# One diffusion trunk layer: the prologue's hand order becomes a table of works

## The chip, the cores and the metric

The kernel runs on one core of a Trainium2 chip. The metric is the device time of one execution in microseconds; lower is better. Engines are named TensorE (PE; PEld is its weight load), VectorE (DVE), ScalarE (ACT), GpSimd (POOL) and SyncE (SP, which issues nearly all DMAs here).

## The reference

One layer for 128 context tokens and 512 latent tokens, 640 rows of 1024 channels. Cut to what the change touches:

```python
ada = silu(c) @ w_ada + b_ada              # c for latent tokens, c_ctx for context tokens
sh1, sc1, g1, sh2, sc2, g2 = split(ada, 6)
u = rms_norm(h, g_pre1) * (1 + sc1) + sh1
z = u @ w_in                               # q 1024, k 256, v 256, then five parts of 1024
k = rms_norm(k, k_norm); keys = concat(cache_k, rope(k)); vals = concat(cache_v, v)
att = softmax(q keys^T / 8) vals           # context reads only context
```

Behind it come a gated convolution, an output projection and a convolutional feed-forward layer, all unchanged. Arithmetic is in float32: a float32 product is made of three products of rounded parts, high x high, high x low and low x high.

## The kernel before

**What the prologue has to make.** Tokens are five tiles t = 0 to 4 of 128 rows (tile 0 is the context), channels eight blocks f = 0 to 7 of 128. The prologue runs from the start to about 57 us and ends with k and v of all tiles, in five PSUM banks, one per tile, each summed over the eight channel blocks. The steps:

- x: load the tile (`XT`), square and sum (ScalarE, L434), factor (`rstd_of`, POOL, L281 and L282), normalise (VectorE, L439, `xn`), turn it by eight TensorE transposes (L446), copy it to `xT` (L452 on ScalarE, L454 on VectorE; two halves of four blocks each).
- small rows: c, c_ctx, b_ada and g_pre1 arrive as rows, are turned (L417), give the silu columns in `s32` (L418, L419) and the feature columns `feat` (L423, L425).
- modulation: for a group of one or two channel blocks the scale and shift columns of `w_ada` are loaded (two loads of 512 KB for a single block, four for a pair), multiplied (L477, 32 narrow matmul instructions for a single block, 64 for a pair), copied (L485), folded by another small product (L490, L493, L497) and put into `scsh` (L502, L504). `modulate` then writes for a block the high part `UH` (ScalarE, L519), the whole `u` (VectorE, L520) and the low part `UL` (VectorE, L523).
- k and v weights: unit u = 0 to 7 is channel block u of 512 columns of `w_in` (256 KB); `cut_upto` makes its high part (ScalarE, L200 or L591) and its low part (VectorE, L201 or L593). Units 8 and 9 are the first two of the q weights (512 KB). There are three slots for raw weights, two of the small units to a slot, and three slots for cut ones.
- product: `kv_mm(f, ts)` adds block f to tiles ts, three matmuls of 128x512 per tile (L235, L236, L237); `kv_first` does block 0 of tiles 0 to 2 (L530).
- rest: cached keys and values, rotary tables times the gains (L666 to L673), the cached keys turned (L546, L552, L553), the rows for the second norm (L681 to L684).

**What sets the order.** The order is written by hand: calls follow one another, and TensorE, ScalarE, VectorE and SP execute in exactly that order (`tc.manual_schedule`). Semaphores between engines come from the tiles' uses. A 32-transposition warm-up (L378) stands first on TensorE. Modulation groups are `((0,), (1,), (2, 3), (4, 5), (6,), (7,))`; those in `JOINT = (0, 3, 4, 5)` are multiplied at once when both parts have landed, groups 1 and 2 in two halves, scale and shift apart.

**What follows.** The attention stage is a list of works with needs (`work`, `Room`) whose order on all engines is the string `PLAN`, played by `follow`. A work names its engine, what it needs, and the rooms (banks, slots) that it uses; a figure behind a number picks the room, a letter picks the engine where there is a choice. PLAN begins with q products on TensorE, squares of k4, k2 and k3 on ScalarE (L871), the rotation of k1 on VectorE (L848, L849) and the addition belonging to it on POOL (L869). Then come projections and the feed-forward layer, which are nearly all matmuls (L1273).

Of the kernel before, what the change touches and what calls it, by code (L numbers as in the profile page):

```python
# [21 lines left out]
D = 1024  # L22
# [69 lines left out]
POOL_WAY = "11111111111111111111111101111100"  # L92

# [19 lines left out]
def trunk_layer(ctx, tc, x_prompt, x_sample, cache_k, cache_v, c, c_ctx, w_ada, b_ada, g_pre1, g_post1, g_pre2,  # L113
# [259 lines left out]
    with tc.tile_pool(name="pro", bufs=2) as pro, tc.manual_schedule(engines={mybir.EngineType.SP}):  # L373
        warm = pro.tile([128, 1], F32, name="warm", bufs=1)
        S.activation(warm, mhalf[:, 0:1], AF.Silu)
        wps = ps1()
        for _ in range(WARM):
            PE.transpose(wps[:, 0:128], ident, ident)  # L378

        def load_rows(srcs, eng):  # L380
            rows = pro.tile([72, 128], F32, tag="rows", name=nm("rows"), bufs=2)
            n = 0
            for src in srcs:
                m = src.shape[0] * src.shape[1] // 128
                eng.dma_start(rows[n:n + m, :], src.rearrange("o (k p) -> (o k) p", p=128))
                n += m
            return rows[0:n, :]

        rows1 = load_rows((c[0:1, :], c_ctx.unsqueeze(0), b_ada.unsqueeze(0), g_pre1), nc.scalar)


        GROUPS = ((0,), (1,), (2, 3), (4, 5), (6,), (7,))
        JOINT = (0, 3, 4, 5)
        araws = {}

        def araw_tile():
            return pro.tile([128, 1024], F32, tag="araw", name=nm("araw"), bufs=4)

        def ada_loads(g, rooms):
            n, c = len(GROUPS[g]), GROUPS[g][0] * 128  # L400
            araws[g] = rooms
            for i, raw in enumerate(rooms):
                o, k = (D, 0)[i // n], i % n * (KT // n)
                nc.sync.dma_start(raw.rearrange("p (k c) -> p k c", c=128 * n),
                                  w_ada[k * 128:(k + KT // n) * 128, o + c:o + c + 128 * n].rearrange("(k p) c -> p k c", p=128))

        XT = region(ra, "r3", [NT, D], F32, "XT")
        for t in range(NT):
            nc.sync.dma_start(XT[:, t, :], xrows(t))
        ada_loads(0, [araw_tile() for _ in range(2)])  # L410
        fetch(1)
        ada_loads(1, [araw_tile() for _ in range(2)])
        fetch(2)

        def features():
            ptr = ps1()
            PE.transpose(ptr[:, 0:72], rows1, ident[0:72, 0:72])  # L417
            S.activation(svec[:, :, 30], ptr[:, 0:8], AF.Silu)  # L418
            S.activation(svec[:, :, 31], ptr[:, 8:16], AF.Silu)  # L419
            return ptr  # L420

        def feature_columns():
            V.tensor_copy(feat[:, 0:72], ptr1[:, 0:72])  # L423
            for o in (8, 32):
                V.tensor_scalar(out=feat[:, F_B + o:F_B + o + 8], in0=feat[:, F_B + o:F_B + o + 8], scalar1=1.0, scalar2=None,  # L425
                                op0=ALU.add)

        xT = Halves(NTOK, F32, "xT")
        xns, rs, xps, pas, es = {}, {}, {}, {}, {}

        def square(t):
            junk = pro.tile([128, D], F32, tag="junk", name=nm("junk"), bufs=1)
            ssq = pro.tile([128, 1], F32, tag="ssq", name=nm("ssq"), bufs=NT)
            S.activation(junk, XT[:, t, :], AF.Square, accum_out=ssq)  # L434
            rs[t] = rstd_of(ssq, 1, 1.0 / D, pro)

        def normal(t):
            xns[t] = pro.tile([128, D], F32, tag="xn", name=nm("xn"), bufs=XB)
            V.tensor_scalar(out=xns[t], in0=XT[:, t, :], scalar1=rs[t], scalar2=None, op0=ALU.mult)  # L439

        def x_turn(t, ks=range(KT)):
            if ks[0] == 0:
                xps[t] = ps2()
            p = xps[t]
            for k in ks:
                PE.transpose(p[:, k * 128:(k + 1) * 128], xns[t][:, k * 128:(k + 1) * 128], ident)  # L446

        def x_copy(t, hf):
            src = xps[t].rearrange("p (k c) -> p k c", c=128)[:, 4 * hf:4 * hf + 4]
            dst = xT.half(hf)[:, :, t * 128:(t + 1) * 128]  # L450
            if t > 0 and hf == 0:
                S.activation(dst, src, AF.Copy)  # L452
            else:
                V.tensor_copy(dst, src)  # L454

        def ada1_mm(g, i):

            n = len(GROUPS[g])
            if i == 0:
                pas[g] = ps1()  # L460
            if g in JOINT and i == 0:
                return
            todo = []
            for kind in (0, 1) if g in JOINT else (i,):
                for f in range(n):
                    for k in range(KT):
                        if g not in JOINT:
                            j, k2 = (2 * f + k // 4, k % 4) if n == 2 else (k % 4, k // 4)
                            last = 3 if n == 2 else 1
                        else:  # L470
                            j, k2 = (2 * kind + f, k) if n == 2 else (2 * kind + k // 4, k % 4)
                            last = 7 if n == 2 else 3
                        raw, m = araws[g][kind * n + k * n // KT], (k % (KT // n) * n + f) * 128
                        todo.append((k2, j, k, raw[:, m:m + 128], last))
            c = 0 if g in JOINT else 128 * i
            for k2, j, k, x, last in sorted(todo, key=lambda z: z[:2]):
                PE.matmul(pas[g][32 * j:32 * j + 32, c:c + 128], s32[:, 32 * k + 30:32 * k + 62], x, start=k2 == 0, stop=k2 == last,  # L477
                          tile_position=(0, 32 * j))

        def ada1_copy(g, a=0, b=2):  # L480
            if a == 0:
                es[g] = pro.tile([128, 256], F32, tag="e", name=nm("e"))
            if g in JOINT:
                a, b = 0, 1
            S.activation(es[g][:, a * 128:b * 128], pas[g][:, a * 128:b * 128], AF.Copy)  # L485

        def ada1_fold(g):
            n, pa, e = len(GROUPS[g]), pas[g], es[g]
            if g in JOINT and n == 2:
                PE.transpose(pa[:, 256:384], e[:, 0:128], ident)  # L490
                at = lambda kind, f: 256 + 32 * (2 * kind + f)
            elif g in JOINT:
                PE.matmul(pa[:, 256:260], e[:, 0:128], sel2, start=True, stop=True)  # L493
                at = lambda kind, f: 256 + 2 * kind
            else:
                for kind in range(2):
                    PE.matmul(pa[:, 256 + 4 * kind:256 + 4 * kind + 2 * n], e[:, kind * 128:kind * 128 + 128], sel2 if n == 2 else sel[:, 0:2],  # L497
                              start=True, stop=True)
                at = lambda kind, f: 256 + 4 * kind + 2 * f
            for i, f in enumerate(GROUPS[g]):  # L500
                c0, c1 = at(0, i), at(1, i)
                V.tensor_scalar(out=scsh[:, f, 0:2], in0=pa[:, c0:c0 + 2], scalar1=feat[:, F_B + 8 + f:F_B + 9 + f],  # L502
                                scalar2=feat[:, F_PRE1 + f:F_PRE1 + 1 + f], op0=ALU.add, op1=ALU.mult)
                V.tensor_scalar(out=scsh[:, f, 2:4], in0=pa[:, c1:c1 + 2], scalar1=feat[:, F_B + f:F_B + 1 + f],  # L504
                                scalar2=None, op0=ALU.add)

        us = {}

        def modulate(f, a=0, b=NTOK, between=()):

            if a == 0:
                us[f] = pro.tile([128, NTOK], F32, tag="u", name=nm("u"))
            u = us[f]
            for i, (s0, s1) in ((1, SEGS[0]), (0, SEGS[1])):
                c, d = max(a, s0), min(b, s1)
                if c < d:

                    x, sc, sh = xT.at(f)[:, c:d], scsh[:, f, i:i + 1], scsh[:, f, 2 + i:3 + i]
                    S.activation(UH[:, f, c:d], x, AF.Identity, scale=sc, bias=sh)  # L519
                    V.tensor_scalar(out=u[:, c:d], in0=x, scalar1=sc, scalar2=sh, op0=ALU.mult, op1=ALU.add)  # L520
            for x in between:
                x()
            V.tensor_tensor(out=UL[:, f, a:b], in0=u[:, a:b], in1=UH[:, f, a:b].bitcast(F32), op=ALU.subtract)  # L523

        def kv_first(ts):

            wh, wl = state["cut"][0].at(0)
# [28 lines left out]
        for t in range(2):  # L556
            square(t)
# [1830 lines left out]
```

## Time and profile before

| | |
|---|---|
| median of 3 runs | 1079.62 us (1079.02 to 1079.99) |
| profiled execution: time / span | 1079.34 us / 1077.5 us |
| mean granted TensorE clock | 0.999 |
| busy over the span: PE, PEld, DVE, ACT, POOL | 99%, 92%, 81%, 54%, 12% |
| HBM read / written | 117.39 MB / 11.44 MB |
| first 40 us: DMA engines' busy share by 4 us | 0.55, 0.91, then 1.08 to 1.18 |
| attention, 57 to 235 us: PE / DVE / ACT busy | 22.5 to 25 of each 25 us at its densest (135 to 160 us) |

How to read it: times are microseconds from the span's start. A line of the timeline gives start, duration, engine, source line, operation, result <- operands, shapes, and in brackets how long the engine had been idle and what ended that. Starts of weight loads (PEld) follow one another more exactly than the matmuls, whose ends are modelled, so TensorE's list is measured by them. A line by stretches (from:to) gives for each engine the busy time and the instructions, then granted clock, DMA share and GB/s.

### The profile page before, as it was taken

What the parts mean: (1) busy time and instruction counts of PE and PEld (TensorE: products, weight loads), DVE (VectorE), ACT (ScalarE), POOL (GpSimd) and SP (SyncE); (2) the same over time, 40 slices, a digit from 0 to 9 for tenths busy, and PEclk for the clock granted to TensorE, in tenths of its full rate; (3) what the DMA queues carried; (4) which work ended last, traced back from release to release, by engine and by line L of the source; (5) the groups of instructions that cost most, each with busy time, mean ns of one, the idle gap of its engine ahead of it and who ended that gap; (6) DMA issues with size and microseconds to landing.
All of it is one profiled execution on the core that took longest, in us unless ns stands there. A gap on an engine that the chain in (4) does not pass through costs nothing.

```text
span 1077.5 us, 20246 instructions
## 1 busy us (share of the span) xinstructions
PE 1062.8 (99%) x8066; PEld 992.2 (92%) x8066; DVE 870.3 (81%) x1328; ACT 583.1 (54%) x1050; POOL 130.8 (12%) x162
## 2 busy tenths in 40 slices
PE   8999999999999999999999999999999999999997
PEld 6788898899999999999998789999999999998886
DVE  5699899855498999896599678889998998989544
ACT  5478999942344554445322466655555654555432
POOL 1087676500000000000000020000000000000001
PEclk9999999999999999999999999999999999999999
DMA  9829999962244333233667634333443443326722
GB/s 316 260 80 175 190 172 180 194 144 60 78 123 124 98 94 94 79 89 100 184 191 257 196 122 137 111 103 104 130 134 112 130 127 106 116 91 210 266 77 98
DMA packets 238444, 152.17 MB, mean 141 GB/s; under 512 B 94602, under 2 KB 215942, under 8 KB 238350
## 3 DMA queue, kind: packets, MB, share of 16 engines
q1 hardware_dynamic: 238238, 150.84, 51.6%
q8 instruction: 63, 1.03, 0.4%
q14 instruction: 31, 0.25, 0.1%
q10 hardware_dynamic: 112, 0.04, 0.0%
HBM read 117.39 MB, written 11.44 MB: 120 GB/s over the span
## 4 chain that ended last, share of the span: by engine, by line
PE 89%; DVE 3%; DMA 3%; ACT 2%; POOL 1%; issue 1%; SPq 0%; DVEq 0%; ACTq 0%; POOLq 0%
PE b L1273 47%; PE b L235 10%; PE b L237 10%; PE b L236 10%; PE s L708 3%; PE s L1072 2%; PE s L1169 2%; DMA araw<-in_w_ada_dram 1%; DMA PT<-P 1%; PE s L235 1%; PE s L237 1%; PE s L477 1%; DMA XT<-in_w_ada_dram 1%; DVE marks L1119 1%; ACT P L1133 1%
## 5 line engine op out<-in xcount | busy, mean ns | idle before, releaser
L1273 PE MATMUL b<-ZBr,whi 128*128 128x320 f32 x688 | 152.2, 309 | 0.0
L1273 PE MATMUL b<-MT,whi 128*128 128x320 f32 x608 | 134.3, 308 | 0.0
L1273 PEld LDWEIGHTS b<-ZBr,whi 128*128 128x128 f32 x688 | 115.0, 188 | 0.1
L1273 PE MATMUL b<-ZBr,wlo 128*128 128x320 f32 x344 | 106.2, 309 | 0.0
L1273 PEld LDWEIGHTS b<-MT,whi 128*128 128x128 f32 x608 | 101.6, 187 | 0.0
L1273 PE MATMUL b<-MT,wlo 128*128 128x320 f32 x304 | 93.6, 308 | 0.0
L1260 ACT ACTIVATE whi<-SUM 128x1024 fp32r<-128x1024 f32 x40 | 42.2, 1055 | 78.4 <-DVE SUM L1812 75.9
L1842 DVE SCALAR_TENSOR_TENSOR Y<-C,cffn,Y 128x642 f32<-128x642 f32 x88 | 77.6, 881 | 0.9
L201 DVE TENSOR_TENSOR wlo<-raw,whi 128x1024 fp32r<-128x1024 f32 (+1 forms) x31 | 34.2, 1102 | 48.2 <-ACT whi L200 47.8
L1273 PE MATMUL b<-ZBT,whi 128*128 128x320 f32 x320 | 71.0, 309 | 0.0
L1273 PE MATMUL b<-UL,whi 128*128 128x320 f32 x228 | 70.7, 310 | 0.0
L1273 PE MATMUL b<-UH,wlo 128*128 128x320 f32 x228 | 70.1, 307 | 0.0
L1260 ACT ACTIVATE whi<-WB 128x1024 fp32r<-128x1024 f32 x38 | 40.1, 1055 | 55.3 <-DVE WB L1367 55.3
L1273 PE MATMUL b<-UH,whi 128*128 128x320 f32 x228 | 69.8, 306 | 0.0
L1273 PEld LDWEIGHTS b<-ZBr,wlo 128*128 128x128 f32 x344 | 64.6, 188 | 0.0
L1281 ACT ACTIVATE p<-b 128x320 f32<-128x320 f32 x78 | 34.2, 438 | 55.5 <-PE b L1273 53.7
L1264 DVE TENSOR_TENSOR wlo<-raw,whi 128x1024 fp32r<-128x1024 f32 (+1 forms) x51 | 50.3, 1017 | 10.3 <-ACT whi L1260 10.3
L1273 PEld LDWEIGHTS b<-MT,wlo 128*128 128x128 f32 x304 | 57.0, 187 | 0.0
L1273 PEld LDWEIGHTS b<-ZBT,whi 128*128 128x128 f32 x320 | 54.2, 188 | 1.5
L1119 DVE TENSOR_REDUCE marks<-s 128x1 f32<-128x640 f32 x64 | 52.0, 816 | 4.1 <-PE s L1072 3.8
L1264 DVE TENSOR_TENSOR wlo<-WB,whi 128x1024 fp32r<-128x1024 f32 x38 | 46.4, 1222 | 8.7 <-ACT whi L1260 8.6
L2250 POOL TENSOR_TENSOR ssqs<-ssqs 128x1 f32<-128x1 f32 x4 | 0.8, 194 | 417.2 <-ACT JK L2243 417.2
(424 smaller groups left out, 3256.8 us busy)
## 6 DMA issues: line engine op xcount, KB each, us to landing
raw<-in_w_in_dram SPq DMA_DIRECT2D x48, 512.0 KB
RAW<-in_w_up_dram SPq DMA_DIRECT2D x40, 512.0 KB
raw<-in_w_down_dram SPq DMA_DIRECT2D x22, 512.0 KB
GA<-in_w_ada_dram SPq DMA_DIRECT2D x16, 512.0 KB
actd<-Y SPq DMA_DIRECT2D x18, 321.0 KB
XT<-in_w_ada_dram SPq DMA_DIRECT2D x9, 512.0 KB
raw<-in_w_att_out_dram SPq DMA_DIRECT2D x8, 512.0 KB
raw<-in_w_conv_out_dram SPq DMA_DIRECT2D x8, 512.0 KB
```

The costliest lines, as they stand in the source:

```text
L201: V.tensor_tensor(out=lo[:, :n], in0=raw, in1=hi[:, :n].bitcast(F32), op=ALU.subtract)
L235: PE.matmul(out, ah, bh, start=start, stop=False)
L236: PE.matmul(out, ah, bl, start=False, stop=False)
L237: PE.matmul(out, al, bh, start=False, stop=stop)
L708: PE.matmul(out, a, b, start=start and n == 0, stop=stop and n == 2, skip_group_check=True)
L1072: PE.matmul(o[h], q_of(hl, i, rows), kk[kx][rows, g, ks], start=m == 0, stop=m == 2, tile_position=(64 * h, 0), skip_group_check=True)
L1119: V.tensor_reduce(out=mk[:, h:h + 1], in_=s_of(), axis=AX.X, op=ALU.max, negate=True)
L1260: S.activation(to[0], raw, AF.Copy)
L1264: V.tensor_tensor(out=lo, in0=raw, in1=hi.bitcast(F32), op=ALU.subtract)
L1273: PE.matmul(out, p[:, ws], q[:, k, :], start=start and k == 0 and n == 0, stop=stop and k == 3 and n == 2, skip_group_check=True)
L1281: S.activation(t, pair[j][b], AF.Copy)
L1842: V.scalar_tensor_tensor(out=y, in0=crows(j)[i][:, d:d + NACT], scalar=cffn[:, 44 * d + o:44 * d + o + 1], in1=y, op0=ALU.mult, op1=ALU.add)
```

## The change

The hand-written calls go. Each step of the prologue becomes a work with its needs and rooms, as in the attention stage, and the order of all engines, of the loads and of the PSUM banks is a second string, `OPENING`, played by the same `follow` (moved up in the file). The groups are now `((0,), (1,), (2,), (3,), (4, 5), (6,), (7,))`: the pair (2, 3) is split, the pair (4, 5) stays, and every group is multiplied at once when all its loads have landed. A pair's four loads stand together and the k and v weights of its blocks behind them. `modulate` is in pieces of its own (`up` on ScalarE, `whole` and `down` on VectorE; five pieces of 128 tokens for block 0, 384 and 256 for the others, where before blocks 3 to 7 had their `UL` in one piece), k and v products are one work per block and tile in any order of tiles, and the low parts of units 8 and 9 are made in two halves each. A copy of x may be on ScalarE or VectorE by the table. PLAN and all that follows it are the same.

The core of the diff (the works for cached keys, tables and the second norm's rows are left out; they do what the calls did):

```diff
+OPENING = """
+0a 1a 5a0 13a0 45a0 46a1 21a0 29a0 37a0 47a0 6a 74a2 75a3 76a0 7a 14a 2a0 4a 8a0 3a 15a 9a0 94a0 11a 16a1 12b 17a1 95a1 96a0
...
+"""
-        GROUPS = ((0,), (1,), (2, 3), (4, 5), (6,), (7,))
-        JOINT = (0, 3, 4, 5)
+        GROUPS = ((0,), (1,), (2,), (3,), (4, 5), (6,), (7,))
...
+        a = work("rows turn", "PE", rows_turn, [rows_in], [fr])
+        sil = work("silus", "ACT", silus, [a], [fr])
+        fea = work("features", "DVE", features, [a], [fr])
...
+            a = work(f"dma x{t}", "SP", x_load, [begin], [xr])
+            a = work(f"square x{t}", "ACT", square, [a], [xr])
+            a = work(f"factor x{t}", "POOL", factor, [a], [xr])
+            a = work(f"normal x{t}", "DVE", normal, [a], [xr, nr])
+            for hf in range(2):
+                a = work(f"turn x{t}", "PE", lambda hf=hf, f=turn_x: f(hf), [a], [nr, pr])
+                turned_x[t, hf] = also(work(f"copy x{t}.{hf}", "DVE", lambda hf=hf, f=x_copy: f(V, hf), [a], [pr]),
+                                       "ACT", lambda hf=hf, f=x_copy: f(S, hf))
...
+            loaded[u] = work(f"dma w{u}", "SP", load, [begin, loaded.get(u - 1)], [raw_room[u]])
+            cut_hi[u] = work(f"hi w{u}", "ACT", hi, [loaded[u], cut_hi.get(u - 1)], [raw_room[u], w_room[u]])
+            cut_lo[u] = [work(f"lo w{u}", "DVE", lambda a=a: lo(a), [cut_hi[u]], [raw_room[u], w_room[u]]) for a in range(0, n, 512)]
...
+                lds.append(work(f"dma ada{g}.{i}", "SP", load_ada, [begin, lds[-1] if lds else None], [room]))
+            for f in fs:
+                weights(f)
...
+                            j, k2, last = (2 * kind + f, k, KT - 1) if n == 2 else (2 * kind + k // 4, k % 4, 3)
...
+            a = work(f"ada{g}", "PE", unit_mm, lds + [sil], ur + [pr])
+            a = work(f"ada copy{g}", "ACT", ada_copy, [a], [pr, er])
+            fold = work(f"ada fold{g}", "PE", ada_fold, [a], [pr, er])
+            for i, f in enumerate(fs):
+                put = work(f"put{f}", "DVE", lambda i=i, f=f, h=ada_put: h(i, f), [fold, fea], [pr])
...
+                    up = work(f"up{f} {a0}", "ACT", up, after)
+                    wh = work(f"whole{f} {a0}", "DVE", whole, after, [ub])
+                    dn = work(f"down{f} {a0}", "DVE", down, [up, wh], [ub])
...
+                    kv_work[f, t] = work(f"kv{f}.{t}", "PE", kv_mm, ready[t] + cut_lo[f] + [kv_work.get((f - 1, t))],
+                                    [kv_rooms[t], w_room[f]])
...
+        follow(OPENING)
+        state["next"] = KT
```

The table read out by names, engine by engine (adaG.i is load i of group G, adaG its product, kvF.T the product of block F and tile T; a figure behind up, whole and down is the first token):

```
SP:  x0 x1 ada0.0 ada0.1 x2 x3 x4 w0 ada1.0 ada1.1 w1 ada2.0 ada2.1 w2 ada3.0 ada3.1 w3 ada4.0 ada4.1 ada4.2 ada4.3
     w4 w5 ada5.0 ada5.1 w6 ada6.0 ada6.1 w7 cv rows2 ck rope gains w8 w9
PE:  rows-turn, turn x0.0 x0.1 x1.0, ada0, turn x1.1, fold0, turn x2 x3 x4, ada1, kv0.0 kv0.2, fold1, kv0.1 kv0.4 kv0.3,
     ada2, kv1.3, fold2, kv1.2 kv1.1, ada3, kv1.4, fold3, kv2.4 kv2.2 kv2.1 kv2.3 kv1.0 kv2.0, ada4, kv3.0, fold4,
     kv3.1 kv3.4 kv3.3 kv3.2 kv4.4 kv4.2 kv4.0 kv4.1, ada5, ada6, kv5.1, fold5, fold6, kv5.0 kv4.3, ck-turn, kv5.4 kv5.3
     kv6.3 kv6.4 kv6.0 kv6.1, rows2-turn, kv5.2 kv6.2 kv7.4 kv7.2 kv7.0 kv7.3 kv7.1
ACT: square x0 x1, silus, copy x0.1 x0.0, square x2, ada-copy0, square x3, up0 128, square x4, up0 0, copy x2.0, hi w0,
     copy x2.1, up0 256, copy x3.1 x4.0, hi w1, up0 512, ada-copy1, up0 384, up1 0 384, hi w2, ada-copy2, up2 0, hi w3,
     up2 384, ada-copy3, up3 0 384, hi w4 w5, ada-copy4, up4 0 384, up5 0, hi w6, up5 384, ada-copy5, ada-copy6,
     up6 384 0, hi w7, ck-hi, up7 0 384, hi w8 w9
DVE: features, normal x0 x1, copy x1.0 x1.1, put0, normal x2, whole0 0 128, down0 128, normal x3, down0 0, normal x4, lo w0,
     whole0 256, down0 256, copy x3.0 x4.1, lo w1, whole0 512 384, down0 512 384, put1, whole1, down1, lo w2, put2, whole2,
     down2 0, lo w3, down2 384, put3, whole3, down3, lo w4 w5, put4 put5, whole4, whole5 384, down4, whole5 0, down5, lo w6,
     put6, gain scale, whole6 384, three tables, down6 384, whole6 0, ck-lo, down6 0, lo w7, put7, table, whole7,
     rows2-put, down7 384 0, lo w8 w9
```

Before, SP's order was x0 to x4, group 0, w0, group 1, w1, the pair (2, 3), w2, w3, the pair (4, 5), w4, w5, group of block 6, w6, group of block 7, w7, the small ones, w8, w9, and the last block's products came in the order of tiles 0 to 4.

522 lines of the change are left out of this document (241 added, 281 removed).

## The prediction

> **What bounds the kernel now.** I read the page first, then the table by stretches, then the timeline and the chain of waits up to 65 us, because the change rewrites only what runs there; the list behind it, PLAN, keeps its order.
>
> ```profile
> span 1077.5 us, 20246 instructions
> PE 1062.8 (99%) x8066; PEld 992.2 (92%) x8066; DVE 870.3 (81%) x1328; ACT 583.1 (54%) x1050; POOL 130.8 (12%) x162
> 12.00:16.00 4.00, 3.28 (x48) 2.60 (x48) 3.21 (x8) 2.13 (x5) 0.97 (x2) 1.00 1.18 306
> 24.00:33.00 9.00, 8.75 (x65) 6.46 (x65) 5.46 (x16) 4.08 (x9) 0.00 (x0) 1.00 1.08 356
> 32.00:36.00 4.00, 4.00 (x74) 3.19 (x73) 1.39 (x3) 0.47 (x2) 0.00 (x0) 1.00 1.13 313
> 36.00:40.00 4.00, 3.95 (x18) 2.89 (x17) 3.29 (x9) 2.74 (x6) 0.00 (x0) 1.00 1.14 307
> ```
>
> The profiled execution took 1079.34 us, 1.84 more than its span; the median of the three timed runs is 1079.62, so 0.28 us is added at the end. About 0.2% (2.2 us) is what a measurement tells from no change. TensorE is busy throughout, and the DMA engines are full up to 40 us. So the prologue has two limits side by side: TensorE's own list, and the bytes that must land before each item of it. The rate depends on what is loaded: 356 GB/s while the loads of the pairs (2,3) and (4,5) pass, whose rows are 256 columns (1 KB), and 307 to 313 while the single groups 6 and 7 pass, whose rows are 128 columns (512 B).
>
> The instants that I compare:
>
> ```profile
> 1.69 6.23 PEld L378 LDWEIGHTS s<-ident 128*128 128x128 f32 x32 [1.69 <-POOL ident masks.py:199]
> 7.89 0.90 PEld L446 LDWEIGHTS s<-ident,xn 128*128 128x128 f32 x8
> 17.30 0.63 PEld L530 LDWEIGHTS s<-whi,UH 128*128 128x128 f32 x3 [0.20 <-issue]
> 33.45 0.12 PEld L477 LDWEIGHTS s<-XT,s 128*32 128x32 f32 x2 [0.36 <-issue]
> 56.67 0.19 PEld L708 LDWEIGHTS s<-whi,UH 128*128 128x128 f32 x1
> 57.55 0.74 POOL L869 TENSOR_TENSOR P<-P,X 128x256 f32<-128x256 f32 x1 [2.54 <-DVE P L849]
> ```
>
> TensorE's weight loads begin the turning of x at 7.89, the k/v products at 17.30, the product of the pair (4,5) at 33.45, and leave the prologue at 56.67. Behind that, VectorE and POOL normalise k and q, beginning at 56.7 and 57.55.
>
> **The first rows of x: 1.6 us later.** The warm-up, unchanged, holds TensorE until 1.69 + 6.23 = 7.92. Before, x0 has been normalised by then. In the new table TensorE's first item is the turn of the small rows and VectorE's first item the feature columns made from it, ahead of "normal x0".
>
> ```profile
> 8.87 0.23 PE L417 MATMUL s<-ident,rows 72*128 72x72 f32 x1
> 10.15 0.76 DVE L439 TENSOR_SCALAR xn<-XT,rstd 128x1024 f32<-128x1024 f32 x1 [0.39 <-POOL rstd L282]
> 10.96 0.85 PEld L446 LDWEIGHTS s<-ident,xn 128*128 128x128 f32 x8 [1.22 <-DVE xn L439]
> 12.29 0.23 DVE L423 COPY feat<-s 128x72 f32<-128x72 f32 x1
> 12.71 0.68 DVE L454 COPY xTb<-s 128x512 f32<-128x512 f32 x1
> ```
>
> So 7.92 + 0.33 (load ahead of it, then 0.23) + 0.05 + 0.42 (features, 12.29 to 12.71) + 0.76 + 0.05 (10.91 to 10.96) = 9.5, against 7.89. Queued behind the feature columns are both first normalisations; TensorE waits for them with nothing else in its list.
>
> **First k/v product: 2.4 us later, with more behind it done.** The two loads of group 0 now go ahead of x2, x3 and x4.
>
> ```profile
> 4.96 0.19 ACT L434 ACTIVATION_READ_ACCUMULATOR junk<-XT 128x1 f32 x1
> 8.06 1.06 ACT L434 ACTIVATE junk<-XT 128x1024 f32<-128x1024 f32 x1 [1.33 <-DMA XT<-in_x_sample_dram]
> 14.18 0.80 PEld L477 LDWEIGHTS s<-araw,s 128*32 128x32 f32 x28 [0.52 <-DMA araw<-in_w_ada_dram]
> 16.72 0.38 PEld L477 LDWEIGHTS s<-araw,s 128*32 128x32 f32 x16 [0.46 <-DMA araw<-in_w_ada_dram]
> 19.73 0.63 ACT L200 ACTIVATE whi<-raw 128x512 fp32r<-128x512 f32 x1 [1.13 <-DMA raw<-in_w_in_dram]
> L281 POOL TENSOR_SCALAR var<-ssq 128x1 f32<-128x1 f32 x5 | 1.5, 292 | 6.8 <-ACT junk L434 6.8
> L282 POOL TENSOR_TENSOR rstd<-var,mhalf 128x1 f32<-128x1 f32 x5 | 2.8, 552 | 0.4
> ```
>
> Before, the third load of 512 KB has landed at 8.03 and the seventh at 14.14, 1.53 us each. Now x4 is the seventh: 14.1. Its square stands in ScalarE's list behind "up0 128" and starts at 14.5; plus 1.25 (square and its read-out), 0.84 on POOL and 0.76 on VectorE it is normalised at 17.4 and turned at 18.4. Then comes the whole product of group 1, whose second load lands between 16.7 and 19.7 (w1, the next but one, has landed at 19.7 in both orders, the same bytes being ahead of it): 18.6 by the pace. Product and transition take 1.0 us. First k/v product: 19.7, against 17.30. The old list spends that time on k/v products and has half of group 1 and all its fold still to do.
>
> **From there to the pair (4,5): 1.8 us of the 2.4 come back.** Prices of TensorE's items, by the starts of weight loads:
>
> ```profile
> 42.36 0.19 PEld L237 LDWEIGHTS s<-whi,UL 128*128 128x128 f32 x1
> 42.91 0.81 PEld L477 LDWEIGHTS s<-XT,s 128*32 128x32 f32 x32 [0.36 <-issue]
> 43.92 0.19 PEld L235 LDWEIGHTS s<-whi,UH 128*128 128x128 f32 x1 [0.20 <-issue]
> 44.03 0.19 PEld L236 LDWEIGHTS s<-wlo,UH 128*128 128x128 f32 x1
> 45.19 0.42 PEld L493 LDWEIGHTS s<-sel,e 128*128 128x128 f32 x2
> 45.53 0.19 PEld L235 LDWEIGHTS s<-whi,UH 128*128 128x128 f32 x1
> 54.30 0.23 PE s L235
> L519 ACT ACTIVATE UH<-xTa,scsh 128x256 fp32r<-128x256 f32 x4 | 2.2, 587 | 0.0
> L485 ACT ACTIVATE e<-s 128x128 f32<-128x128 f32 x6 | 1.6, 274 | 10.6 <-PE s L477 10.6
> ```
>
> A k/v product of one tile is 3 x 0.23 = 0.695 us. A whole single group costs 43.92 - 42.36 - 0.23 - 0.12 (the short step behind it, 43.92 to 44.03) = 1.2; a fold about 0.22. The new list has 15 k/v products (10.4), groups 2 and 3 (2.4) and three folds (0.65): 13.5 us. Waits on top: group 3's product for its load, and fold 3, which stands behind "hi w3" and so behind w3's landing in ScalarE's list. With w1 landed at 19.7, 512 KB of 512-byte rows take 1.7 us (307 to 313 GB/s), of 1 KB rows 1.48 (356), w units 0.74: group 3 at 27.2, w3 at 28.0, the pair's last load at 33.9. TensorE comes to group 3 at 19.7 + 8 x 0.695 + 1.2 + 2 x 0.22 = 26.9, with the transition at 27.1 (0.1 lost), to fold 3 at 28.8, while w3's cut (0.63), "up2 384" (0.59) and the copy (0.27), each beginning 0.1 before the last one ends, end at 29.3 (0.5 lost). The pair's product: 19.7 + 13.5 + 0.6 + 0.3 (transition) = 34.1, just behind its load, against 33.45. The old stretch also holds the other half of group 1, two longer folds and waits for loads; from there the 1.8 us come back.
>
> Here the trace and the Trainium skill differ. "DMA: Bandwidth & Descriptors", section Specifications, puts line rate at 512 B and above. By that, splitting (2,3) into single loads costs nothing, the loads come about 0.8 us earlier, and the sum would end near 1079.4 us; this trace's 307 to 313 against 356 GB/s speak against it, by 1.7 against 1.48 us a load.
>
> **From the pair to the end of the prologue: nothing.** The work is the same (25 k/v products, pair, two singles, folds, cached keys). Before it takes 56.67 - 33.45 = 23.2 with one stall:
>
> ```profile
> 39.71 0.19 PEld L237 LDWEIGHTS s<-whi,UL 128*128 128x128 f32 x1 [0.48 <-DVE UL L523]
> 45.74 0.28 DVE L502 TENSOR_SCALAR scsh<-s,feat 128x2 f32<-128x2 f32 x1
> 52.55 0.82 DVE L523 TENSOR_TENSOR UL<-u,UH 128x640 fp32r<-128x640 f32 x1 [0.43 <-ACT UH L519]
> 55.54 1.22 DVE L201 TENSOR_TENSOR wlo<-raw,whi 128x1024 fp32r<-128x1024 f32 x1
> 56.72 0.41 DVE L848 TENSOR_TENSOR X<-s,tabk 128x256 f32<-128x256 f32 x1
> 57.80 0.42 DVE L873 TENSOR_REDUCE ssqs<-Z 128x4 f32<-128x260 f32 x1 [0.34 <-ACT Z L871]
> 56.83 0.25 PE s L237
> ```
>
> New: 23.2 - 0.36 + 0.1 (first product of group 4 behind its "down") + 0.1 (two small turns now apart) gives 57.1, 0.5 later than before. Covers that could fail: group 6's last load lands at 33.9 + 1.5 (w4, w5) + 3.4 (group 5) + 0.7 (w6) + 3.4 = 42.9 and is asked for at 34.1 + 2.0 (pair) + 6.3 (nine products) + 0.3 (fold, stall) + 1.2 (group 5) = 43.9. VectorE's run from "put6" to "down7 0" took 45.74 to 53.37 before, with some 0.9 us of gaps; the cached keys' and small rows' part (0.9) now lies in it, so again about 7.7: 46.1 (group 6, a product and the fold after 43.9) to 53.8, 0.5 before TensorE needs it. SP's list needs no room that is freed late: each reuse (x rows, group tiles) is free some us before its place in the stream. The tables, gains and cached keys move within VectorE's list but stay under products.
>
> **The boundary: 0.1 more.** PLAN starts VectorE with k1's rotation. Before, it started when VectorE was free (55.54 + 1.22 = 56.7). Now kv7.1 is TensorE's last item, so the rotation waits for it: 57.1 + 0.4 (before, the last product ended at 56.83 + 0.25 = 57.08, 0.41 behind 56.67) = 57.5, 0.8 later. k4 and k2 are done early, so ScalarE's squares no longer hold VectorE 0.34 us: VectorE is 0.4 late, POOL (first item behind that rotation) 0.75, TensorE 0.5. From 57 us VectorE and POOL have no gap worth that, so it stays. I take 0.6: 1079.34 + 0.6 = 1079.9, and with 0.28, **1080.2 us**.
>
> Bounds: all rows exist but the landing times. With every load 1 us earlier TensorE's list closes up and ends at 56.4 (-0.3); 1 us later costs 1.0 more. That gives 1079.1 to 1081.7 for the forecast.
>
> **Rivals.** *Loads later (slower).* TensorE, ScalarE and VectorE each wait in list order for w1, group 3, w3 and the pair, with nothing to overtake. If a run of 512-byte rows alone moves at 250 GB/s, not 307 (no trace shows four such loads in a row), the four loads of groups 2 and 3 take 8.4 us instead of 6.8, and the two of group 5 and two of group 6 lose as much again, of which 1.0 is covered. It passes 0.2% when the pair's last load lands after 35.6; with 1.6 there and 0.6 later, 1080.2 + 2.2 = 1082.4, up to 1083.5. For it: DMA engines full, 306 in the mixed stretch. Against: 307 to 313 with w units between. Chance 0.25.
>
> *The list closes up (faster).* No gap behind the first k/v product, the 0.34 us wait gone and the early squares used: 1079.62 - 0.3 - 0.3 = 1079.0, still no change. To pass -2.2 the first k/v product would have to start at 17.6, a microsecond before group 1's second load can have landed by the pace; 1077.0. Chance 0.09, mostly for an effect in the stretch behind 57 us that I do not see.
>
> **Numbers.** No change 0.66, slower 0.25, faster 0.09. The range 1078.6 to 1082.8 takes the forecast's own (1079.1 to 1081.7), the gap-free case, and most of the slower rival.
>
> **What would show it.** First turn of x at 9.5; first k/v product near 19.7; pair at 34.1 with TensorE waiting little; last k/v product near 57.1; "k1 rotation" starting on TensorE's end, not on VectorE's. Wrong if the pair's last load lands after 35.6, if kv starts before 18.5, or if the stretch behind 60 us differs by more than the prologue does.

## The result, and the profile after

The changed kernel takes 1082.03 us (median; 1080.57 to 1083.80) against 1079.52 for the one before: ratio 1.0027, interval 1.0017 to 1.0038, 2.5 us slower. Measured once more beside the experiments it is 1080.98 against 1078.95, ratio 1.0019 (1.0010 to 1.0028), 2.0 us slower: at the border of what can be told from no change. The forecast was 1080.2 with a range to 1082.8: the range holds the time, but the likeliest case, "no change" with 0.6 us of loss, is not what came. Some 1.4 to 1.9 us are missing from the sum.

The profiled execution of the changed kernel is the slowest of its runs (1083.80, span 1082.0), so it shows the loss enlarged. First its page:

```profile
span 1082.0 us, 20268 instructions
PE 1063.2 (98%) x8064; PEld 993.2 (92%) x8064; DVE 871.2 (81%) x1343; ACT 586.2 (54%) x1059; POOL 129.9 (12%) x162
```

TensorE's busy time is 0.4 us above that of before, the span 4.5: TensorE has no more work, it stands still. Where, says its list of weight loads (start, duration, what it waited for), here at the instants that the prediction named:

```profile
7.86 0.14 PEld L490 LDWEIGHTS s<-ident,rows 72*128 72x128 f32 x1 [1.35 <-issue]
9.40 1.29 PEld L529 LDWEIGHTS s<-ident,xn 128*128 128x128 f32 x12 [1.40 <-DVE xn L523]
19.96 0.19 PEld L672 LDWEIGHTS s<-whi,UH 128*128 128x128 f32 x1 [0.20 <-issue]
27.96 0.80 PEld L618 LDWEIGHTS s<-araw,s 128*32 128x32 f32 x28 [0.43 <-DMA araw<-in_w_ada_dram]
34.54 0.91 PEld L618 LDWEIGHTS s<-XT,s 128*32 128x32 f32 x34 [0.36 <-issue]
...
49.60 0.19 PEld L672 LDWEIGHTS s<-wlo,UH 128*128 128x128 f32 x1
52.63 0.29 PEld L672 LDWEIGHTS s<-whi,UL 128*128 128x128 f32 x1 [2.84 <-DVE UL L660]
52.79 0.33 PEld L672 LDWEIGHTS s<-whi,UH 128*128 128x128 f32 x1
53.22 0.33 PEld L672 LDWEIGHTS s<-wlo,UH 128*128 128x128 f32 x1
...
61.44 0.19 PEld L753 LDWEIGHTS s<-whi,UH 128*128 128x128 f32 x1
```

The first turn of x (9.40), the first k/v product (19.96) and the pair (34.54) are within 0.5 us of the forecast; in between, group 3's last load ends TensorE's wait at 27.96, some 0.8 later than forecast (27.2). Then, in the first product of block 6, TensorE waits 2.84 us for VectorE's `UL`. Behind the wait the loads follow one another every 0.43 us instead of 0.23. TensorE leaves the prologue at 61.44, not at 57.1. VectorE's list and SP's queue say what it waited for; the last four lines are from the kernel before:

```profile
46.25 0.28 DVE L633 TENSOR_SCALAR scsh<-s,feat 128x2 f32<-128x2 f32 x1 [3.36 <-PE s L629]
47.53 0.20 DVE L706 TENSOR_SCALAR tabq<-tabq 128x64 f32<-128x64 f32 x1 [0.87 <-DMA tabq<-in_q_norm_dram]
50.73 0.29 DVE L711 TENSOR_TENSOR tabk<-araw,tabk 128x128 f32<-128x128 f32 x1 [2.68 <-DMA tabk<-in_k_norm_dram]
52.15 0.42 DVE L660 TENSOR_TENSOR UL<-u,UH 128x256 fp32r<-128x256 f32 x1
44.38 0.43 SPq L695 DMA_DIRECT2D tabq<-in_q_norm_dram  x1
45.30 0.33 SPq L695 DMA_DIRECT2D tabk<-in_k_norm_dram  x1
```

```profile
42.61 0.43 SPq L654 DMA_DIRECT2D tabq<-in_q_norm_dram  x1
43.09 0.42 SPq L654 DMA_DIRECT2D tabk<-in_k_norm_dram  x1
48.15 0.19 DVE L666 TENSOR_SCALAR tabq<-tabq 128x64 f32<-128x64 f32 x1
49.33 0.28 DVE L669 TENSOR_TENSOR tabk<-araw,tabk 128x128 f32<-128x128 f32 x1
```

The gains of the two norms, 32 KB each, are issued 1.8 and 2.2 us later than before (44.38 against 42.61, 45.30 against 43.09), because SP's list reaches them later. And the new table of VectorE wants tabk first: it waits for it at 48.05 (50.73 less 2.68), where before it came to it at 49.33. Before, neither waited. The trace also shows when the gains had landed. Among these loads only the rope rows and, behind them, the gains move in packets of 256 bytes; the last such packet ends at 50.38 here and at 48.41 in the kernel before. Behind tabk stands "down6 384", the `UL` of block 6 (52.15), and behind that TensorE. The DMA rate from 40 to 52 us in 40 slices of 0.3 us shows the small loads passing:

```profile
GB/s 207 294 323 314 297 283 232 232 236 311 231 206 178 194 256 150 96 95 304 394 179 40 56 26 66 36 34 43 56 176 259 285 355 359 375 396 379 256 178 140
```

From 46.3 to 48.7 the engines move 26 to 66 GB/s, though a load of 512 KB has been issued behind the gains at 45.75. The last new thing is the granted clock, the column before the last two (from:to, width, busy us of PE, PEld, DVE, ACT and POOL, clock, DMA share, GB/s):

```profile
14.00:16.00 2.00, 1.57 (x8) 1.31 (x8) 1.90 (x6) 1.67 (x4) 1.60 (x3) 0.68 1.16 292
16.00:18.00 2.00, 2.00 (x10) 1.94 (x10) 1.49 (x4) 1.82 (x4) 0.55 (x1) 0.50 1.12 321
24.00:33.00 9.00, 8.80 (x92) 6.50 (x87) 6.22 (x17) 4.57 (x10) 0.00 (x0) 1.00 1.05 327
52.00:54.00 2.00, 1.37 (x3) 1.16 (x4) 2.00 (x7) 0.00 (x0) 0.00 (x0) 0.57 0.08 26
54.00:56.00 2.00, 2.00 (x7) 1.52 (x6) 2.00 (x9) 0.83 (x2) 0.00 (x0) 0.58 0.03 5
```

It is about half for two stretches of 3 to 4 us, in the turning of x and behind the wait.

The theory (T1): the gains come too late for VectorE's list, which stands at the first table, and TensorE pays for it. Rivals: late loads of 512-byte rows (R1, the slower rival of the prediction), the boundary (R2: k1's rotation behind TensorE's last item), the half clock (R3, and H for its cause).

### The profile page after: what moved, and what is told of

Read it like the earlier page. It is cut to its first block, busy times and chain, and to the rows that moved or that the text cites. A ratio compares the mean times of both kernels' runs of the same rounds, so it can differ in the third digit from the quotient of the medians.

```text
span 1082.0 us, 20268 instructions
## 1 busy us (share of the span) xinstructions
PE 1063.2 (98%) x8064; PEld 993.2 (92%) x8064; DVE 871.2 (81%) x1343; ACT 586.2 (54%) x1059; POOL 129.9 (12%) x162
## 4 chain that ended last, share of the span: by engine, by line
PE 89%; DVE 3%; DMA 3%; ACT 2%; POOL 1%; issue 1%; SPq 0%; DVEq 0%; ACTq 0%; POOLq 0%
PE b L1283 47%; PE b L248 10%; PE b L250 10%; PE b L249 10%; PE s L753 4%; PE s L1082 2%; PE s L1179 2%; PE s L672 1%; DMA araw<-in_w_ada_dram 1%; PE s L1171 1%; DVE marks L1129 1%; DMA raw<-in_w_in_dram 1%; PE b L1907 1%; ACT P L1143 1%; PE s L529 1%
## 5 line engine op out<-in xcount | busy, mean ns | idle before, releaser
L1274 DVE TENSOR_TENSOR wlo<-raw,whi 128x1024 fp32r<-128x1024 f32 (+1 forms) x51 | 50.4, 1020 | 13.5 <-ACT whi L1270 13.5
L214 DVE TENSOR_TENSOR wlo<-raw,whi 128x1024 fp32r<-128x1024 f32 x22 | 26.9, 1224 | 38.8 <-ACT whi L213 38.7
L1270 ACT ACTIVATE whi<-raw 128x1024 fp32r<-128x1024 f32 (+1 forms) x51 | 43.6, 893 | 15.1 <-DMA raw<-in_w_o_dram 12.1
```

The lines of the kernel that those rows point to most:

```text
L214: V.tensor_tensor(out=lo[:, :n], in0=raw, in1=hi[:, :n].bitcast(F32), op=ALU.subtract)
L1270: S.activation(to[0], raw, AF.Copy)
L1274: V.tensor_tensor(out=lo, in0=raw, in1=hi.bitcast(F32), op=ALU.subtract)
```

## The experiments

Medians are of 11 runs; each ratio is to runs of the kernel before that were taken beside them.

**The gains asked for earlier or used later.** Two edits take the same wait away from its two ends.

```diff
 SP (early gains):   ... w4 w5
+gains
 ada5.0 ada5.1 w6 ada6.0 ada6.1 w7 cv rows2 ck rope
-gains
 w8 w9
```

> The changed kernel with one edit: the load of the small gains (tabq, tabk and the norms' rows) is issued behind the loads of group 5 instead of behind the cached keys and the rope rows. All lists of the other engines stay. Theory T1 (the late gain loads hold VectorE's list at the first table, TensorE stands 2.8 us in block 6 and then runs at half clock): VectorE's wait for tabk (2.68 us) and tabq (0.87) go, TensorE's 2.84 us wait at kv6.3 goes, the granted clock at 52 to 56 us is 1.0, the last k/v weight load is near 57.0 instead of 61.44, and the median is 1079.5 to 1080.3, some 2 us below the changed kernel's 1082.0. Rival R1 (512-byte rows load more slowly, everything is late): the last k/v load stays after 60 and the time at 1081.5 or more. Rival R2 (the boundary: k1's rotation stands behind TensorE's last item): the prologue ends at 57, but the time stays at 1081.5 or more. Rival R3 (the early half clock, 14 to 20 us): no change either.

```diff
 VectorE (late tables):  ... put6
-gain scale
 whole6 384
-three tables
 down6 384 ... put7
-table
 whole7 rows2-put down7 384 0
+gain scale, four tables
 lo w8 w9
```

> The changed kernel with one edit: the scaling of the gains and the four table products stand in VectorE's list behind the last turn into sign and magnitude of group 7 (down7 0) instead of ahead of block 6's; all loads stay as they are. T1: the gain loads are as late as before (47.5 and 50.7), but nothing that TensorE needs is queued behind them, so TensorE's 2.84 us wait at kv6.3 and the half clock go, the last k/v weight load is near 57, and the median is 1079.5 to 1080.5. If instead the late landing itself (busy DMA engines, SP's list) costs the time, the end stays at 61 and the median near 1082. If the tables are now too late for the first normalisation of k, POOL and VectorE start some tenths later and the gain is smaller by these.

(With early gains, the two loads stand behind w5 and ahead of group 5's loads, as the list shows, not behind them as the expectation says.)

Measured: early gains 1079.06, ratio to before 1.0001 (0.9993 to 1.0010); late tables 1079.42, ratio 1.0004 (0.9995 to 1.0013). The timeline with early gains, and in the last two lines with late tables:

```profile
46.13 0.18 DVE L707 TENSOR_SCALAR tabq<-tabq 128x64 f32<-128x64 f32 x1
46.58 0.28 DVE L712 TENSOR_TENSOR tabk<-araw,tabk 128x128 f32<-128x128 f32 x1
48.00 0.42 DVE L661 TENSOR_TENSOR UL<-u,UH 128x256 fp32r<-128x256 f32 x1
56.92 0.19 PEld L754 LDWEIGHTS s<-whi,UH 128*128 128x128 f32 x1
57.36 0.42 DVE L859 TENSOR_TENSOR X<-s,tabk 128x256 f32<-128x256 f32 x1 [0.53 <-PE s L673]
46.83 0.42 DVE L661 TENSOR_TENSOR UL<-u,UH 128x256 fp32r<-128x256 f32 x1 [0.22 <-ACT UH L651]
56.87 0.19 PEld L754 LDWEIGHTS s<-whi,UH 128*128 128x128 f32 x1
```

With early gains there is no wait for them, TensorE leaves at 56.92, and the rotation starts at 57.36. With late tables tabk is issued at 44.49, and the last 256-byte packet ends at 48.63; block 6's `UL` is made at 46.83 all the same, TensorE leaves at 56.87, and the loss is gone. So a late landing alone costs nothing that shows; it costs because TensorE's block 6 stands behind it: T1 holds from both sides, and R1, R2 and R3, which would have left the time near 1082, do not explain it.

**How late is late.** Two places earlier, and one place later:

```diff
 SP (before the keys):   ... w7 cv rows2
+gains
 ck rope
-gains
 w8 w9
```

> The changed kernel with the gain loads moved by two places only, ahead of the cached keys and the rope rows (2 x 128 KB and 256 KB) that stood ahead of them. T1: issued near 40.7 instead of 43.8 to 45.3 and landed before VectorE asks at 46.1, so the waits for tabq and tabk go; the rope rows are issued 0.9 us later and land near 46.5, where VectorE needs them for the first table, a wait of 0 to 0.7 us that block 6 can cover; median 1079.0 to 1079.6. If the loads of gains are slow in themselves by 5 us whatever stands ahead of them, tabq and tabk still wait 0 to 0.3 us. If the rope rows are the later ones, the wait moves to them and the median stays above 1080.

```diff
 SP (later gains):   ... ck rope
-gains
 w8
+gains
 w9
```

> The changed kernel with the small gain loads one place later in SP's list, behind the 512 KB load w8, which stood behind them. T1 (what lands late holds VectorE's list, and TensorE pays it one for one): 512 KB pass ahead of the gains, 1.5 us at the pace of 343 GB/s, so tabk lands 1 to 2 us later than in the changed kernel, TensorE's wait at kv6.3 is longer by as much, and the median is 1083 to 1084.5. If the changed kernel's wait is from another cause that ends about then, one place more in the queue changes nothing: near 1082.

Ahead of the keys: 1079.13, ratio 1.0006 (0.9997 to 1.0015). Two places are enough; VectorE's first table waits 0.76 us for the rope rows instead, until 47.93, and the products ahead of block 6's `UL` cover all but 0.2 of it.

Later gains: 1081.20, ratio 1.0019 (1.0010 to 1.0028), only 0.2 above the unaltered kernel measured beside it, where T1 expected 1 to 2.5 more. That number missed, and the trace says why:

```profile
45.24 0.50 SPq L696 DMA_DIRECT2D tabq<-in_q_norm_dram  x1
45.78 0.43 SPq L696 DMA_DIRECT2D tabk<-in_k_norm_dram  x1
49.28 0.20 DVE L707 TENSOR_SCALAR tabq<-tabq 128x64 f32<-128x64 f32 x1 [2.54 <-DMA tabq<-in_q_norm_dram]
49.87 0.29 DVE L712 TENSOR_TENSOR tabk<-araw,tabk 128x128 f32<-128x128 f32 x1
51.77 0.19 PEld L673 LDWEIGHTS s<-whi,UL 128*128 128x128 f32 x1 [1.90 <-DVE UL L661]
```

tabk is issued 0.5 us later than in the first profile and has landed 0.9 earlier (by 49.87 against 50.73). I had counted the 512 KB ahead in the queue; what counts is the time from issue to landing, and in these profiles that varies by more than one place in the list is worth. TensorE's wait follows it, 1.90 us here. The chain T1 names is the same; its size is not a matter of bytes ahead.

**The unaltered kernel again.**

> The changed kernel, unaltered, once more, with another profile, as the mark for the runs beside it. T1: the median is 1081 to 1082.5 again; the profile shows VectorE waiting at the first table for tabk and TensorE at kv6.3 for VectorE; the length of that wait (2.84 us in the first profile, 1 to 2 us where dummies were added) follows the landing of tabk, and the granted clock behind it is low only if the pause is long. If the first profile was an exception, the wait is missing and the median is near 1080.

1080.98, ratio 1.0019 (1.0010 to 1.0028). Its profile:

```profile
43.82 0.35 SPq L695 DMA_DIRECT2D tabk<-in_k_norm_dram  x1
48.65 0.29 DVE L711 TENSOR_TENSOR tabk<-araw,tabk 128x128 f32<-128x128 f32 x1 [1.72 <-DMA tabk<-in_k_norm_dram]
50.55 0.19 PEld L672 LDWEIGHTS s<-whi,UL 128*128 128x128 f32 x1 [1.36 <-DVE UL L660]
52.20 0.19 PEld L672 LDWEIGHTS s<-whi,UL 128*128 128x128 f32 x1 [0.42 <-DVE UL L660]
52.00:54.00 2.00, 2.00 (x8) 1.27 (x8) 2.00 (x9) 0.90 (x3) 0.00 (x0) 1.00 0.04 5
20.50 0.19 PEld L672 LDWEIGHTS s<-whi,UH 128*128 128x128 f32 x1 [0.20 <-issue]
34.21 0.81 PEld L618 LDWEIGHTS s<-XT,s 128*32 128x32 f32 x32 [0.36 <-issue]
```

The wait is there, 1.36 + 0.42 = 1.8 us, and the clock behind it is full. So the 2.84 us with half clock of the first profile are the longest that the profiles show of a wait that varies with tabk's landing; 1.8 us of wait stand against 1.9 us between this median and that of early gains (1.3 us between the spans of the two profiles, 1078.5 and 1077.2). Three of the eleven runs took 1083.0 to 1083.3; why is open. One of them had a mean granted clock of 0.999, which no profile with a low stretch has, so the low clock alone does not explain them.

This profile also says which end of the wait moved. Its last 256-byte packet ends at 48.34, as before the change (48.41); with dummies late and early, below, at 48.29 and 48.82. The gains land here about when they did before the change. But VectorE comes to the first table at 46.93 (48.65 less 1.72) instead of 49.33. So the usual loss is an early use more than a late load; the first profile had both.

**The clock.** Dummy transposes keep TensorE busy in the late wait, or in the early gaps:

```diff
+        def first_fill(number, n, out):
+            eng, do = works[number].ways[0]
+            def both_():
+                for _ in range(n):
+                    PE.transpose(out()[:, 0:128], ident, ident)
+                do()
+            works[number].ways[0] = (eng, both_)
+        first_fill(189, 24, lambda: kv_tiles[2][:, 512:1024])   # late: ahead of kv6.3
...
+        first_fill(9, 12, early_bank)                           # early: ahead of turn x0.0,
+        first_fill(52, 5, early_bank)                           # fold0
+        first_fill(25, 11, early_bank)                          # and turn x2.0
```

> The changed kernel with 24 dummy transposes of 128 columns added to TensorE's list ahead of kv6.3, into a half of a PSUM bank that is not used at that time; their result is used by nobody. The wait for the tables stays. Theory H (a pause of some 2.8 us drops the granted clock for the next 3.4 us): the dummies keep TensorE going for about 2.6 us of the wait, the clock at 52 to 56 us is near 1.0 instead of 0.57, the load pitch behind the wait is 0.23 instead of 0.43 us, the last k/v load is near 59.9 instead of 61.4, the median is some 1.6 us below 1082.0, near 1080.4. Rival (the low clock is not from the pause but from the load on the chip or the start of the program): the clock stays at 0.57, the dummies only add, the median is 1082.0 or more.

> The changed kernel with dummy transposes of 128 columns added to TensorE's list in the early gaps: 12 ahead of the turn of x0, 5 ahead of the first fold, 11 ahead of the turn of x2, into a bank that is not used then. Theory H: the granted clock at 14 to 20 us (0.68, 0.50, 0.96 in the changed kernel) is near 1.0, the turn of x3 and x4 takes 1.7 instead of 2.7 us, and the first k/v product starts at 19.3 to 19.6 instead of 19.96. T1: since TensorE then waits for the tables at kv6.3 in any case, the end of the prologue stays near 61 and the median within 0.5 us of 1082.0. Rival R3 (the early half clock is what costs the 2.5 us): the median falls to 1080.

Late: 1080.99, the median of the unaltered kernel (1080.98), where H expected 1080.4; the clock is 1.00 in both profiles from 52 us on. The dummies themselves hold TensorE 2.74 us (48.35 to 51.09), and it waits for nothing behind them. So this run cannot tell H from its rival: the low clock at 52 us shows in the first profile only, and the loss is there without it.

Early: 1080.52, ratio 1.0019 (1.0010 to 1.0027), and the clock at 14 to 20 us is 1.00; the first k/v product starts at 19.48, as expected. The median misses T1's "within 0.5 us of 1082.0", but it is not clear of the unaltered kernel's 1080.98, and TensorE still waits 2.4 us for `UL` in this profile: R3 is not borne out. Without early dummies the clock was full in six of the ten profiles of these kernels and half in four (the expectation of the last run below says three of six; at that time it was three of eight). That this half clock does not reach the end is shown by two pairs of profiles. The unaltered kernel's second one had it (0.58 and 0.57 at 16 to 20 us), began the k/v products at 20.50, 0.76 later than with early gains (19.74), and came to the pair at 34.21, 0.16 earlier (34.37). With late tables it was there too (0.52 and 0.63), and TensorE left the prologue at 56.87, with early gains and a full clock at 56.92.

The ten traces also show what goes with it. The transposes of the warm-up follow one another every 0.21 us and then every 0.11, and the first record of a full clock stands at that change. It comes at 4.42, 4.50, 5.85 and 6.08 in the four profiles with the low stretch and between 6.56 and 7.41 in the six without. Each early low stretch begins 10.24 us behind it and lasts 3.41 us. With early dummies the change came at 5.49, among those of the four, and the clock stayed full (in the last run below at 6.16, just outside). So the low clock goes with the moment at which the clock became full, and the one profile with dummies in that span speaks for the gaps as its other condition; no run sets this moment on purpose. The Trainium skill, TensorE: Matmul & The Clock Gate, part 1, has the gate decide over a free-running window of some 3.4 us, so that the phase of a run matters. The records of the traces agree: the low stretches last 3.41 us each time, the late one too (52.29 to 55.70), 10.24 is three times that, and the low clock comes and goes between runs of one list. No run here tests it.

**The boundary.** Early gains, and kv7.1 second in block 7:

```diff
 TensorE:   ... kv7.4
+kv7.1
 kv7.2 kv7.0 kv7.3
-kv7.1
```

> The changed kernel with the gain loads behind those of group 5 (as in the run of early gains, 1079.06) and in addition kv7.1 second in block 7 of TensorE's list instead of last, so that k1, the row tile that VectorE rotates first behind the prologue, is ready early. R2 (the boundary costs, as the prediction took it: the rotation waits for TensorE's last product, VectorE 0.4 late, POOL 0.75): the rotation starts at 56.8 when VectorE is free, not at 57.4, without the wait of 0.53 us on TensorE, and the median falls by 0.4 to 0.6 to about 1078.5. Rival (the list behind has room, the 0.6 us are hidden): the rotation starts earlier, the median stays within 0.25 of 1079.06.

1078.99, ratio 1.0000 (0.9991 to 1.0009).

```profile
56.55 0.42 DVE L859 TENSOR_TENSOR X<-s,tabk 128x256 f32<-128x256 f32 x1
57.38 0.74 POOL L880 TENSOR_TENSOR P<-P,X 128x256 f32<-128x256 f32 x1 [3.20 <-DVE P L860]
```

VectorE's rotation starts 0.81 earlier than with early gains alone and POOL at 57.38, and the time is the same within 0.1 us. The rival holds: 0.8 us at this place are hidden by the list behind.

**The row size.** Early gains, and the four loads of groups 2 and 3 in 1-KB rows. They bring as many bytes, but other columns, so blocks 2 and 3 are made from other weights than the layer's; only the time is of use here.

```diff
-                def load_ada(i=i, room=room, n=n, c=fs[0] * 128):
+                def load_ada(i=i, room=room, n=n, g=g, c=fs[0] * 128):
...
+                    if g in (2, 3):
+                        nc.sync.dma_start(unit_of(room).rearrange("p (k c) -> p k c", c=256),
+                                          w_ada[0:512, o + c:o + c + 256].rearrange("(k p) c -> p k c", p=128))
+                        return
```

> The changed kernel with the early gains, and the loads of groups 2 and 3 take rows of 1 KB instead of 512 B: the same bytes (4 x 512 KB) from the same matrix, but 512 rows of 256 columns in place of 1024 rows of 128, so groups 2 and 3 are worked out from other weights (this part of the computation is changed). The prediction's pace (1.7 us for a load of 512-byte rows, 1.48 for 1-KB rows): the four loads land 0.9 us earlier, the rate at 24 to 33 us rises from about 335 to above 350 GB/s, TensorE's wait of 0.46 us for group 3 goes, the pair (4,5) is taken some 0.5 to 0.8 us earlier than 34.4, the last k/v product is near 56.3 and the median 0.4 to 0.8 below 1079.06. By the Trainium skill, DMA: Bandwidth & Descriptors, section Specifications (line rate at 512 B and above): no change in rate or time.

1078.28, ratio 0.9992 (0.9983 to 1.0001), 0.7 below the run with k1 early measured beside it (1077.50 to 1079.04 against 1078.62 to 1079.59). Against the kernel before the interval still reaches 1. By stretches, first that run with 512-byte rows, then this one:

```profile
18.00:20.00 2.00, 2.00 (x40) 1.59 (x39) 1.87 (x6) 1.37 (x4) 0.00 (x0) 1.00 1.21 292
20.00:24.00 4.00, 4.00 (x37) 3.11 (x39) 3.70 (x12) 2.30 (x7) 0.00 (x0) 1.00 1.17 309
```

```profile
18.00:20.00 2.00, 2.00 (x41) 1.63 (x41) 1.87 (x5) 1.36 (x3) 0.00 (x0) 1.00 1.10 351
20.00:24.00 4.00, 4.00 (x25) 3.07 (x29) 3.86 (x13) 2.85 (x8) 0.00 (x0) 1.00 1.08 357
33.62 0.91 PEld L623 LDWEIGHTS s<-XT,s 128*32 128x32 f32 x34 [0.36 <-issue]
```

357 against 309 GB/s, the wait for group 3's load is gone, and the pair is taken at 33.62 instead of 34.06. The pace of the prediction holds: 512 KB at these rates take 1.70 and 1.47 us, where it had 1.7 and 1.48. By the Trainium skill (DMA: Bandwidth & Descriptors, Specifications: line rate from 512 B) nothing should have moved; here the measurement decides.

**Covering the waits around group 3.** Early gains, k1 early, and:

```diff
 TensorE:   kv1.2 kv1.1
+kv1.4
 ada3
-kv1.4
+kv1.0
 fold3 kv2.4 kv2.2 kv2.1 kv2.3
-kv1.0
 kv2.0
 ScalarE:   ... up2 0
+up2 384
 hi w3
-up2 384
 VectorE:   ... down2 0
-lo w3
 down2 384
+lo w3
```

> The run with early gains and k1 early (median 1078.99), with the two waits around group 3 covered: in TensorE's list kv1.4 goes ahead of group 3's product and kv1.0 behind it, ahead of its fold; in ScalarE's list 'up2 384' goes ahead of 'hi w3', in VectorE's list 'lo w3' behind 'down2 384', so that nothing of block 2 stands behind the landing of w3. If TensorE's list is what sets the end of the prologue, as the prediction summed it, the waits of 0.34 to 0.46 us (load of group 3) and 0.49 us (copy of group 3) go, the pair is taken near 33.4 instead of 34.06, the last k/v product comes 0.6 to 0.8 us earlier, and the median is 1078.2 to 1078.5. Rival (the pair's last load then sets the pair): a wait on DMA appears ahead of the pair at 33.5 to 33.9 and the gain is 0.2 or less.

> The kernel of the group-3 run with the 28 dummy transposes of the early-fill run in TensorE's gaps at 8 to 18 us. The granted clock at 14 to 20 us, half in three of the six profiles of these kernels without early dummies and full in the one with them, stays 1.0. If the early half clock reaches the end of the prologue in some executions now that the waits behind it are gone, the median is 0.2 to 0.4 below that of the group-3 run and the spread smaller; if the loads or VectorE's chain from x4 set the first k/v product anyway, the two medians agree within 0.2.

1078.91, ratio 1.0004 (0.9995 to 1.0013), and with the early dummies 1078.96, ratio 1.0004 (0.9995 to 1.0013). The waits for group 3 go and others come on the loads behind it: 0.3 us for the pair in the one profile, 1.1 us for group 6 in the other, until 44.33 (the prediction had this load at 42.9). The two medians agree within 0.1, as expected if the early half clock does not reach the end. As the rival said, up to there the bytes set the pace, not the order of the lists. No version here is faster than the kernel before beyond the interval.

## Why the prediction was right, and where it was not

| | forecast | changed kernel, first profile | with early gains |
|---|---|---|---|
| first turn of x | 9.5 | 9.40 | 9.58 |
| first k/v product | 19.7 | 19.96 | 19.74 |
| pair (4,5) | 34.1 | 34.54 | 34.37 |
| "put6" | 46.1 | 46.25 | 45.81 |
| TensorE leaves the prologue | 57.1 | 61.44 | 56.92 |
| k1's rotation | 57.5 | 61.87 | 57.36 |
| time against before | +0.6 us | +2.5, again +2.0 | +0.25 (ratio 1.0001) |

*The step that failed* is one sentence of "From the pair to the end": "The tables, gains and cached keys move within VectorE's list but stay under products." They are priced at nothing, and cost 1.9 us in the median (2.84 and more in the first profile). That sentence names a cover, the products ahead of them, but not what is queued behind them, "down6 384" and so TensorE's block 6; nor that VectorE now comes to the first table 1.3 us (first profile) to 2.4 us (second) earlier, while tabk is issued 2.2 and 0.7 later. The use could have been worked out from the place in the list, and the issue from the loads' pace; the landing is in no sum, but the trace of before had it: by 48.41, 0.9 ahead of the use at 49.33 and behind the 46.9 to 48.1 at which VectorE asks now. For SP's list I asked only whether each item finds its room free, not when the small loads at its end land.

*The clock.* The prediction did not price a lower clock: before, it was full. In the first profile the eight loads behind the wait cost about 1.4 us more (seven steps of 0.43 instead of 0.23). With 2.84 of wait and 0.17 at the pair this makes 4.4 of the 4.5 us between 61.44 and 56.92. In the second profile this term is nothing.

*First rows, first k/v product, pair.* Right within 0.5 us, and with early gains within 0.3. For the first turn in the first profile that was luck: the warm-up ended at 6.76, not at 7.92, and what held the first item until 7.89 was the small rows' load (1.14 us of wait). With early gains the warm-up did end near 8.1. That a later start of the k/v products comes back until the pair held: even with the start at 20.50 the pair was at 34.21. My reason was half of it. The lists' waits do close up, but it is the loads that set the pace behind: taking the two waits of the list away gained nothing, quicker loads gained 0.7 us.

*Group 3's wait* was 0.43 us where I had 0.1, at its own load; fold 3's was 0.47 where I had 0.5.

*The boundary and "so it stays".* The rotation does wait for TensorE (0.53 us). But starting it 0.81 earlier changed nothing to be seen, and with the gains early the kernel equals the one before although its rotation starts at 57.36 and not at 56.72. The 0.6 us that I carried to the end are, by the medians, 0 to 0.25; the intervals of 0.9 us don't settle more.

*The rivals.* "Loads later" named the right sign by the wrong mechanism: its sign for itself was the pair's last load after 35.6, and the pair was under way at 34.54. So it is luck that the range, widened for this rival, holds the time. Without the gains' wait, the change is what the likeliest case said, no change.

## What to carry to other kernels

When an order is rewritten, go through the small loads at the end of the queue too: for each, the time of issue and of landing against the first instruction that uses it, and then what is queued behind that instruction on its engine. A tiny load with nothing to gain from waiting belongs early in the queue, and its user behind whatever the bottleneck engine needs; either of the two was enough here. And where the bytes set the pace, as here up to group 6, a better order of the lists only moved the wait to the next load.

## What the hardware showed

- A load of 32 KB that copies one row of 256 B to 128 partitions took long when it stood at the end of the queue: tabk 5.4 us from issue to use in the first profile (45.30 to 50.73), 4.8 in the second (43.82 to 48.65), and at most 4.1 with later gains (45.78 to 49.87). Before the change it had landed by 48.41, 5.3 us behind its issue at the most. While the last of the two passed in the first profile, the engines moved 26 to 66 GB/s. The cause of the variation stays open.
- Rows of 512 B moved at 309 GB/s where rows of 1 KB, as many bytes at the same place of the queue, moved at 357.
- The granted clock fell to about 0.5 at 14 to 20 us, between gaps of 1.4 us and less, in some profiles and not in others with the same list ahead of it: in the four of ten in which the warm-up reached the full clock by 6.08 us, and in none in which it did so from 6.56 on. It lasted 3.41 us each time. With a wait of 2.84 us it fell once, with waits of 1.4, 1.9 and 2.0 it did not; what decides there is open.
